# Six chunks instead of four for the prompt alone in the first gated MLP, and a wider pace for the sample stream

## The chip, the cores and the metric

The kernel runs on one core of one Trainium2 chip. Its engines work side by side, each in the order in which its own instructions stand: PE (TensorE, matrix products), DVE (VectorE), ACT (ScalarE), POOL (GpSimd) and SP (SyncE, which issues most of the transfers). Transfers run on 16 DMA engines that all queues share. The metric is the device time of one execution in microseconds (us); less is better.

## The reference

A two-layer decoder trunk is run over a prompt of 512 tokens and over 8 sample sequences of 8 new tokens each (64 rows), with the same weights. Layer 0 has stick-breaking attention, in which the samples also attend to 2048 cached positions in pages of 128; layer 1 has a diagonal complex state-space layer (S5). Both end in a gated MLP with a causal convolution of width 3.

```python
def trunk(x, past_kv, ssm_prev, conv_prev, p):
    ...
        h = rms_norm(x, p["norm_mix"][i])
        if i % 2 == 0:
            y, k, v = attn_mixer(h, ..., past_k, past_v)      # samples: 16 pages of 128 keys each
        else:
            y, fr, fi = s5_mixer(h, ...)
        x = x + y
        h = rms_norm(x, p["norm_ffn"][i])
        y, cs = conv_ffn(h, w_up, conv_w, conv_b, w_down, prev)
        x = x + y

def conv_ffn(h, w_up, conv_w, conv_b, w_down, prev):
    a, b = jnp.split(h @ w_up, 2, axis=-1)                    # (rows, 2816) each
    padded = jnp.concatenate([prev, a], axis=1)
    c = conv_b + conv_w[0] * padded[:, 0:s] + ...             # width 3
    return (silu(c) * b) @ w_down, padded[:, s:]
```

D_MODEL is 1024 and D_FF 2816, so an MLP has 22 chunks of 128 hidden features.

## The kernel before, in words

**Precision.** A product in float32 is made of three float32r products: weights (`whi`, `wlo`) and activations (`hT`, `g`, `o_hi` and `o_lo`) are split into a high and a low part. A weight unit of 128x1024 is loaded by SP into one of three `raw` buffers (`load_unit`, L150); ACT copies it to `whi` (L139) and DVE subtracts to get `wlo` (L140). Four pairs of them form a ring.

**The stream.** `sample_cache` (L396) walks over the cached pages of the samples, two sequences at a time, in 64 steps. A step loads two pages of keys (`kp`, SP's queue, two buffers) and of values (`vp`, POOL's queue, two buffers), turns the keys on DVE (`kt`, L427), makes the scores on PE (`z`, L448), turns the weights (`z<-ident,sg`, L473) and multiplies with the values (`po`, L483). Each step is four pieces. `accompany(stream, WEAVE)` puts one piece behind every 2400 cycles of products; `tick`, which every product loop calls, counts them. This sets the place of a piece in the program. The program is then ordered by a list scheduler: each engine takes what the scheduler holds ready, earlier program text first, so pieces can move ahead of their place where an engine would be idle, and fall back to their place where it is full.

**The stages.** Queries are projected for all heads; then eight pairs of heads are projected, normed and attended (`project_pair`, `norm_pair`, `prompt_pair`); then the attention output is multiplied with `w_o` for the prompt (`psg<-w,o`, 192 products of 512 columns); then comes the first MLP, `ffn(0, ...)`. The stream runs beside all of them.

**The first MLP.** `PLAN0` lists its groups as (both, first chunk, number of chunks). A group multiplies its chunks up (`up`, products of L880 to L882 into `up` or, for the first parts of chunks 0 and 1, into `dn`), and then down (`gemm`, L267 to L269, into `dn`, four prompt tiles of 128 rows times two halves of the output). Where `both` is false the group holds the 512 prompt columns alone, because the samples' rows are not there yet. During its down products `sample_joins` is run: the stream is finished, the new tokens are attended (`sample_new`: `psc`, `zn`, `pwn`, `pon`, `pot`), their attention output `soT` is multiplied with `w_o` (`pso`, 32 products), added and normed, and turned into `hT` and `sT` (`up<-ident,h` with 64 rows). Chunks of later groups hold 576 columns, prompt and samples. The samples' part of the first chunks is made up later by `sample_group`, with the samples as the stationary operand and the weights, loaded a second time, as the moving one; its pieces are taken one behind each chunk from chunk `SSTART` on. Beside the later chunks runs the preparation of the S5 layer (`s5_prepare`, "aside"), mostly DVE and POOL work in steps, `ASTEPS` (44) of them spread by `beside` over the chunks up to `AEND` (20).

Lines to know: L139 and L140 splits; L880 to L882 up products; L267 to L269 down products; L264 and L265 products with the samples as stationary operand; L1031 the samples' up products of `sample_group`; L219 transposes into `hT`.

Of the kernel before, what the change touches and what calls it, by code (L numbers as in the profile page):

```python
# [9 lines left out]
F32 = mybir.dt.float32  # L10
F32R = mybir.dt.float32r
# [3 lines left out]
ALU = mybir.AluOpType  # L15
AX = mybir.AxisListType

P = 128
# [3 lines left out]
NT = SEQ // P  # L22
DB = 8
# [20 lines left out]
GUNITS = 0, 2, 4, 6  # L44
WEAVE, NPERIOD, IPERIOD = 2400, 6000, 1200
BIG = 4
ASTEPS, AEND = 44, 20
SSTART = 14
GROUPS = [[4], [0, 1], [2, 3]]
# [14 lines left out]
AHEAD = 2  # L64
PLAN0 = [(False, 0, 4), (True, 4, 6), (True, 10, 4), (True, 14, 4), (True, 18, 4)]
PLAN1 = [(True, 0, 6), (True, 6, 6), (True, 12, 6), (True, 18, 4)]
# [25 lines left out]
def hybrid_kernel(  # L92
# [179 lines left out]
    def sample_rows(pool, ps, out, tag, bufs):  # L272

        lo = pool.tile([P, 512], F32, name="slo", tag=tag, bufs=bufs)
        S.copy(lo[:NS], ps[NS:2 * NS])
        V.tensor_tensor(out, ps[:NS], lo[:NS], ALU.add)

# [632 lines left out]
    def ffn(l, start, plan, then=None, between=None, aside=None):  # L910
# [3 lines left out]
        with ExitStack() as fctx:  # L914
            pool = fctx.enter_context(pool_(name=f"ffn{l}", bufs=2))
            ups = fctx.enter_context(pool_(name=f"ffn{l}_u", bufs=2, space=PSUM))
            dps = fctx.enter_context(pool_(name=f"ffn{l}_d", bufs=3, space=PSUM))
            extra = {}

            def bank():  # L920
# [35 lines left out]
            def beside(ins, c):  # L956

                with tc.issue_after(ins.ins), tc.issue_after(last_mm["PE"].ins):
                    while steps["n"] * (AEND - plan[1][1]) < ASTEPS * (c - plan[1][1]):
                        next(steps["of"], None)  # L960
                        steps["n"] += 1
# [56 lines left out]

            def sample_group(sx, sT, c0):

                cs = slice(c0, c0 + 4)
                out = []
                for part in range(2):
                    f0 = part * FF + c0 * P
                    ps = down_bank(3)
# [9 lines left out]
                    sample_rows(pool, ps, t[:NS], "cv", 2)  # L1035
                    ps = down_bank(3)
                    for c in range(4):
                        T.transpose(ps[:, c * NS:(c + 1) * NS], t[:NS, c * P:(c + 1) * P], ident[:NS, :NS])
                    src = ps[:, :4 * NS].rearrange("p (c b s) -> p c b s", c=4, s=DS)
                    if part == 0:  # L1040
                        ap = pool.tile([P, 4, DB, 2 + DS], F32, name="sap", tag="apad")
                        for c in range(4):
                            G.tensor_copy(ap[:, c, :, 0:2], hist[:, :, c0 + c].rearrange("p (b j) -> p b j", j=2))
                        S.copy(ap[:, :, :, 2:], src)
                        for c in range(4):
                            G.tensor_copy(cst[:, 2:, c0 + c].rearrange("p (b j) -> p b j", j=2), ap[:, c, :, DS:])
                        cv = sx.tile([P, 4, DB, DS], F32, name="scv", tag="scv")
                        t = pool.tile([P, 4, DB, DS], F32, name="sct", tag="cv")

                        def per(w):  # L1050
                            return cw[:, w, cs, None, None].to_broadcast([P, 4, DB, DS])

# [7 lines left out]
                V.tensor_tensor(cv, src, cv, ALU.mult)  # L1060
                g = sx.tile([P, 4, P], F32R, name="sg", tag="sg2")
# [40 lines left out]
            def sample_joins():  # L1102
# [15 lines left out]
                aside_ps = fctx.enter_context(pool_(name="aside_ps", bufs=1, space=PSUM, side="right"))  # L1118
                yield (chain(*(sample_group(sx, sT, c) for both, c, _ in plan if not both)),
                        aside(fctx.enter_context(pool_(name="aside", bufs=2, side="right")),  # L1120
                              lambda: aside_ps.tile([P, 512], F32, name="as", tag="as")))

            for both, c0, ncg in plan:
# [15 lines left out]
                if not both:  # L1139
                    joining = sample_joins()  # L1140
                    x = next(joining)
                    for n in range(2):
                        units = down_units(c0, ncg, n)
                        for i in range(NT):
                            if (n, i) in JOINAT:
                                x = next(joining)
                            ps = down_bank(0)
                            gemm([(i, ps)], lhs, units, 2, ncg)
                            add(i, ps, halves[n], False)
                    early, steps["of"] = x  # L1150
                elif last:
# [612 lines left out]
```

## Time and profile before

| what | value |
|---|---|
| time of the runs, median of 3 | 1870.84 us (1863.1 to 1871.09) |
| time of the profiled execution | 1861.24 us |
| its span from first to last instruction | 1859.6 us, so 1.6 us lie around it |
| PE busy, share of the span | 1696.9 us, 91% |
| DVE busy | 1157.4 us, 62% |
| ACT busy | 740.9 us, 40% |
| POOL busy | 279.4 us, 15% |
| moved by DMA | 297.30 MB, 160 GB/s in the mean |

Busy PE is not PE at its peak: the records of matmuls overlap, and the clock that the chip grants PE changes (PEclk, in shares of 2.4 GHz). So shares over the whole span say little here; the stages differ, and the rows below are read stage by stage.

### The profile page before, as it was taken

The page shows a single profiled execution, that of the slowest core. Times are in us where ns is not written, and L with a number is a line of the kernel's source. Part 1 is how long each engine was busy: PE and PEld are TensorE (multiplying, and loading weights), DVE is VectorE, ACT ScalarE, POOL GpSimd, SP SyncE. Part 2 cuts the span into 40 slices and gives each one's busy share as a digit, 9 for nine tenths or more (in the row PEclk, how much of TensorE's full clock was granted, in tenths as well). Part 3 has the DMA queues.
Part 4 walks back from the last instruction along what each step waited for, and adds up shares of the span by engine and source line. Part 5 has one row for each costly group of instructions (what it writes and reads, how often), then busy time and mean ns, then how long its engine had stood idle before and what let it go on. Part 6 is the DMA issues. An engine that isn't in the chain of part 4 may idle for free. (4 is left out here: it accounts for less than half of the span.)

```text
span 1859.6 us, 34131 instructions
## 1 busy us (share of the span) xinstructions
PE 1696.9 (91%) x12765; PEld 1425.3 (77%) x12765; DVE 1157.4 (62%) x2132; ACT 740.9 (40%) x1526; POOL 279.4 (15%) x455
## 2 busy tenths in 40 slices
PE   5979878898788879997999899899999999999999
PEld 4867655566445668796888889789888989989897
DVE  7356755676775567799577887665446544444443
ACT  4324443454453336433244534454433423323231
POOL 3011000111111100066032332011010100000000
PEclk8989988898788989999999999999999999999999
DMA  8399989999999973623375736455322222232221
GB/s 250 97 251 267 252 213 252 257 254 264 275 257 257 255 191 95 181 69 117 113 146 150 199 108 172 120 161 169 118 82 73 91 81 80 81 91 80 82 80 64
DMA packets 278713, 297.30 MB, mean 160 GB/s; under 512 B 54424, under 2 KB 197745, under 8 KB 278548
## 3 DMA queue, kind: packets, MB, share of 16 engines
q1 hardware_dynamic: 258642, 226.66, 45.7%
q0 software_dynamic: 18752, 67.41, 12.9%
q8 instruction: 101, 1.65, 0.4%
q10 hardware_dynamic: 1154, 1.05, 0.2%
q14 instruction: 64, 0.52, 0.1%
HBM read 268.93 MB, written 26.13 MB: 159 GB/s over the span
## 5 line engine op out<-in xcount | busy, mean ns | idle before, releaser
L880 PE MATMUL up<-hT,whi 128*128 128x256 f32 (+2 forms) x1344 | 406.7, 303 | 14.1 <-DVE gf L1000 5.4
L140 DVE TENSOR_TENSOR wlo<-raw,whi 128x1024 fp32r<-128x1024 f32 x203 | 255.2, 1260 | 254.8 <-ACT whi L139 239.4
L881 PE MATMUL up<-hT,whi 128*128 128x256 f32 (+2 forms) x1344 | 402.9, 300 | 0.0
L882 PE MATMUL up<-hT,wlo 128*128 128x256 f32 (+2 forms) x1344 | 402.8, 300 | 0.0
L139 ACT CAST whi<-raw 128x1024 fp32r<-128x1024 f32 x206 | 215.5, 1049 | 335.5 <-PE up L881 152.3
L880 PEld LDWEIGHTS up<-hT,whi 128*128 128x128 f32 x1344 | 256.3, 191 | 22.4 <-DVE gf L1000 7.1
L881 PEld LDWEIGHTS up<-hT,whi 128*128 128x128 f32 x1344 | 256.5, 191 | 3.6 <-issue 0.8
L882 PEld LDWEIGHTS up<-hT,wlo 128*128 128x128 f32 x1344 | 256.2, 191 | 1.6 <-issue 0.2
L427 DVE STREAM_TRANSPOSE kt<-kp 128x1024 f32<-128x1024 f32 x128 | 152.2, 1224 | 156.0 <-DMA kp<-in_cache_k_dram 131.9
L422 POOL DMA_DIRECT2D vp<-in_cache_v_dram x128 | 67.8, 530 | 572.1 <-PE po L483 447.7
L267 PE MATMUL dn<-whi,g 128*128 128x512 f32 x352 | 137.3, 401 | 9.3 <-DVE xres L1077 5.3
L268 PE MATMUL dn<-wlo,g 128*128 128x512 f32 x352 | 140.6, 400 | 0.0
L269 PE MATMUL dn<-whi,g 128*128 128x512 f32 x352 | 139.0, 398 | 0.0
L448 PE MATMUL z<-kt,Qall 128*32 128x128 f32 x2048 | 89.0, 305 | 52.2 <-DVE kt L427 46.6
L448 PEld LDWEIGHTS z<-kt,Qall 128*32 128x32 f32 x2048 | 61.2, 121 | 77.7 <-issue 38.0
L986 POOL COPY cst<-apad 128x2 f32<-128x2 f32 x44 | 39.3, 894 | 510.3 <-ACT apad L974 510.3
L267 PE MATMUL psg<-whi,hT 128*128 128x256 f32 (+1 forms) x320 | 103.2, 325 | 0.0
L268 PE MATMUL psg<-wlo,hT 128*128 128x256 f32 (+1 forms) x320 | 101.9, 319 | 0.0
L269 PE MATMUL psg<-whi,hT 128*128 128x256 f32 (+1 forms) x320 | 100.7, 318 | 0.0
L457 ACT ACTIVATE left<-z,nbias_r 128x128 f32<-128x128 f32 x128 | 40.1, 364 | 146.8 <-PE z L448 128.8
L483 PE MATMUL po<-vp,wT 128*32 128x256 f32 x1024 | 79.8, 432 | 16.5 <-DMA vp<-in_cache_v_dram 11.9
L267 PEld LDWEIGHTS dn<-whi,g 128*128 128x128 f32 x352 | 66.2, 189 | 27.0 <-DVE xres L1077 6.2
(484 smaller groups left out, 3329.9 us busy)
## 6 DMA issues: line engine op xcount, KB each, us to landing
kp<-in_cache_k_dram SPq DMA_DIRECT2D x256, 256.0 KB, 9.1
vp<-in_cache_v_dram POOLq DMA_DIRECT2D x128, 512.0 KB, 9.2
raw<-in_ffn_w_up_dram SPq DMA_DIRECT2D x96, 512.0 KB, 4.4
raw<-in_ffn_w_down_dram SPq DMA_DIRECT2D x48, 512.0 KB, 3.3
raw<-in_attn_w_qkv_dram SPq DMA_DIRECT2D x64, 128.0 KB, 3.6
raw<-in_attn_w_o_dram SPq DMA_DIRECT2D x16, 512.0 KB, 5.4
raw<-in_ssm_w_glu_dram SPq DMA_DIRECT2D x32, 256.0 KB, 3.3
f_scr<-ca SPq DMA_DIRECT2D x8, 512.0 KB
```

Source lines behind the costliest of these rows:

```text
L139: S.copy(hi, src)
L140: eng.tensor_tensor(lo, src, hi.bitcast(F32), ALU.subtract)
L267: T.matmul(ps, x[0], whi, start=st, stop=False)
L268: T.matmul(ps, x[0], wlo, start=False, stop=False)
L269: T.matmul(ps, x[1], whi, start=False, stop=sp_)
L422: last_dma[G] = G.dma_start(vps[i][:, s], cache_v[0, bass.ds(r, 1)].rearrange("o k h d -> (o k) (h d)"))
L427: V.transpose(kts[i, a].rearrange("p b c k -> p b (c k)"), kps[i][:, :, a * 256:(a + 1) * 256])
L448: T.matmul(z[32 * h:32 * h + 32, a * P:(a + 1) * P].rearrange("p (k b) -> p b k", b=4), Qall[:, b, 8 * a + 2 * h + half, :], kt[:, :, 2 * ...
L483: T.matmul(po[32 * h:32 * h + 32, a].rearrange("p (s j d) -> p s j d", s=2, j=2), wT[:, a, 32 * h:32 * h + 32], v[:, a, h], start=m0 == NP ...
L880: T.matmul(ps[:, :t1 - t0], w[0][:, k, :], hi, start=k == 0, stop=False)
L881: T.matmul(ps[:, :t1 - t0], w[0][:, k, :], lo, start=False, stop=False)
L882: last_mm["PE"] = T.matmul(ps[:, :t1 - t0], w[1][:, k, :], hi, start=False, stop=k == KC - 1)
```

## The change

`PLAN0` gets a second group for the prompt alone, chunks 4 and 5; the first group for both starts at chunk 6 and has four chunks. The samples join in the last group for the prompt alone (`joins`). `sample_group` takes the number of its chunks as an argument, so that a group of two is made up as well, with weight units of half the size. A piece of the stream is put behind every 2900 cycles of products instead of 2400. The pieces of `sample_group` are taken from chunk 9 on instead of 14. The 44 steps beside the chunks are counted from chunk 6 instead of 4, and so stand beside 14 chunks instead of 16.

```diff
-WEAVE, NPERIOD, IPERIOD = 2400, 6000, 1200
+WEAVE, NPERIOD, IPERIOD = 2900, 6000, 1200
-SSTART = 14
+SSTART = 9
-PLAN0 = [(False, 0, 4), (True, 4, 6), (True, 10, 4), (True, 14, 4), (True, 18, 4)]
+PLAN0 = [(False, 0, 4), (False, 4, 2), (True, 6, 4), (True, 10, 4), (True, 14, 4), (True, 18, 4)]
...
+            first_both = min(c for both, c, _ in plan if both)
...
-                    while steps["n"] * (AEND - plan[1][1]) < ASTEPS * (c - plan[1][1]):
+                    while steps["n"] * (AEND - first_both) < ASTEPS * (c - first_both):
...
-            def sample_group(sx, sT, c0):
+            def sample_group(sx, sT, c0, m4):
...
-                        w = rows_unit(ffn_w_up[l], u * 256, 2, f0, 512)
+                        w = rows_unit(ffn_w_up[l], u * 256, 2, f0, m4 * P)
...
-                    gemm([(NT, ps)], lambda k, i: g[:, k], down_units(c0, 4, n), 2, 4)
+                    gemm([(NT, ps)], lambda k, i: g[:, k], down_units(c0, m4, n), 2, m4)
...
                 if not both:
-                    joining = sample_joins()
-                    x = next(joining)
+
+                    joins = c0 == max(c for b, c, _ in plan if not b)
+                    if joins:
+                        joining = sample_joins()
+                        x = next(joining)
                     for n in range(2):
                         units = down_units(c0, ncg, n)
                         for i in range(NT):
-                            if (n, i) in JOINAT:
+                            if joins and (n, i) in JOINAT:
                                 x = next(joining)
                             ps = down_bank(0)
                             gemm([(i, ps)], lhs, units, 2, ncg)
                             add(i, ps, halves[n], False)
-                    early, steps["of"] = x
+                    if joins:
+                        early, steps["of"] = x
```

**What it moves.** The lines of the changed kernel are one higher from L275 on, and more further down (z is L449 there, po L484). On every engine the order is the same as before until about the 34th step of the stream, in the middle of the pairs. The first place is PE in the middle of the products with `w_o`. Before, a step of the stream stood between any two dozen of them:

```order
L269 MATMUL psg<-whi,o_lo 128x512
L267 MATMUL psg<-whi,o_hi 128x512
L483 MATMUL po<-vp,wT 32x256 x8
L448 MATMUL z<-kt,Qall 32x4x32 x16
L473 MATMUL z<-ident,sg 128x128 x2
L268 MATMUL psg<-wlo,o_hi 128x512
L269 MATMUL psg<-whi,o_lo 128x512
```

Now all 192 of them follow each other but for a few rows at their beginning and their end; these are the end:

```order
L269 MATMUL psg<-whi,o_lo 128x512
L484 MATMUL po<-vp,wT 32x256 x3
L449 MATMUL z<-kt,Qall 32x4x32 x16
L474 MATMUL z<-ident,sg 128x128 x2
L484 MATMUL po<-vp,wT 32x256 x8
L908 MATMUL up<-ident,nat 128x88
L881 MATMUL dn<-hT,whi 128x256
```

Counted over PE's whole order, 53 of the 64 `po` steps stood ahead of the products with `w_o` before, nine more ahead of the first MLP's first product (seven of them among the products with `w_o`), and the last two beside chunk 0. Now 52 stand ahead of `w_o`, one is cut in two among its products (five rows of eight, and the three that are seen above), one comes behind them, and ten follow the first MLP's first product, spread over the up products of chunks 0 to 3 and the down products of the first group. The last of them comes just ahead of chunk 4.

DVE shows the same place by the adds of the products with `w_o` into the residual rows (`xres`). Before, the stream's key turns and scans stood between them:

```order
L140 TENSOR_TENSOR wlo<-raw,whi 128x1024
L818 TENSOR_TENSOR xres_91<-psg,xres_91 128x512
L427 STREAM_TRANSPOSE kt<-kp 128x1024 x2
L463 SCALAR_TENSOR_TENSOR left<-left 128x129 x2
L818 TENSOR_TENSOR xres_92<-psg,xres_92 128x512
```

Now there are none:

```order
L140 TENSOR_TENSOR wlo<-raw,whi 128x1024 x2
L819 TENSOR_TENSOR xres_91<-psg,xres_91 128x512
L819 TENSOR_TENSOR xres_92<-psg,xres_92 128x512
L819 TENSOR_TENSOR xres_93<-psg,xres_93 128x512
L819 TENSOR_TENSOR xres_94<-psg,xres_94 128x512
```

The second place is PE where the samples join: `pot` turns their attention output, `pso` multiplies it with `w_o`, `dn` are down products of the group in which they join. Before, 18 down products stood between the last `pot` and the first `pso`, and the `pso` came by fours among the down products:

```order
L269 MATMUL dn<-whi,g 128x512
L264 MATMUL pso<-whi,soT 128x512
L265 MATMUL pso<-wlo,soT 128x512
L264 MATMUL pso<-whi,soT 128x512
L265 MATMUL pso<-wlo,soT 128x512
L267 MATMUL dn<-whi,g 128x512
```

Now the group has half as many down products; the last `pot` is followed at once by all 32 `pso`, and 24 down products are left behind them, before the samples' rows are turned:

```order
L268 MATMUL dn<-wlo,g 128x512
L269 MATMUL dn<-whi,g 128x512
L570 MATMUL pot<-ident,osum 128x128 x4
L264 MATMUL pso<-whi,soT 128x512
L265 MATMUL pso<-wlo,soT 128x512
L264 MATMUL pso<-whi,soT 128x512
```

## Rows read from the trace of the kernel before

**Rows 1.** Stretches: from:to, length, busy (count) PE, PEld, DVE, ACT, POOL, clock, DMA, GB/s
```profile
466.00:584.00 118.00, 92.57 (x929) 51.44 (x929) 79.46 (x139) 51.06 (x135) 14.26 (x27) 0.79 1.00 266
...
593.70:625.90 32.20, 32.20 (x301) 24.55 (x300) 20.67 (x32) 11.92 (x32) 4.23 (x8) 1.00 1.08 259
...
668.00:685.00 17.00, 16.64 (x151) 14.31 (x151) 6.81 (x29) 2.55 (x8) 0.89 (x4) 0.83 0.47 135
...
783.80:796.80 13.00, 13.00 (x99) 12.94 (x98) 11.62 (x53) 4.91 (x11) 2.11 (x6) 1.00 0.28 83
...
795.00:890.00 95.00, 81.85 (x502) 74.12 (x501) 89.75 (x198) 29.71 (x45) 58.65 (x73) 0.95 0.32 103
890.00:1190.00 300.00, 284.80 (x1862) 255.90 (x1860) 220.26 (x340) 129.72 (x236) 78.04 (x87) 0.99 0.55 141
```

**Rows 2.** PE in order of time, the stream's value products at the end of the pairs
```profile
566.12 1.07 PE L483 MATMUL po<-vp,wT 128*32 128x256 f32 x16 [2.25 <-DMA vp<-in_cache_v_dram]
...
575.12 1.94 PE L483 MATMUL po<-vp,wT 128*32 128x256 f32 x16
```

**Rows 3.** PE in order of time, steps of the stream around products with w_o
```profile
584.01 0.78 PE L267 MATMUL psg<-whi,o_hi 128*128 128x512 f32 x1
...
601.83 1.07 PE L483 MATMUL po<-vp,wT 128*32 128x256 f32 x16
602.72 1.06 PE L448 MATMUL z<-kt,Qall 128*32 128x128 f32 x32
603.70 0.44 PE L473 MATMUL z<-ident,sg 128*128 128x128 f32 x2
...
604.45 0.39 PE L269 MATMUL psg<-whi,o_lo 128*128 128x512 f32 x1
...
609.58 0.39 PE L267 MATMUL psg<-whi,o_hi 128*128 128x512 f32 x1
609.90 1.07 PE L483 MATMUL po<-vp,wT 128*32 128x256 f32 x16
...
653.97 1.91 PE L219 MATMUL psg<-ident,h 128*128 128x128 f32 x8
655.53 0.78 PE L267 MATMUL psg<-whi,o_hi 128*128 128x512 f32 x1
...
659.20 1.05 PE L448 MATMUL z<-kt,Qall 128*32 128x128 f32 x32
...
665.37 1.93 PE L483 MATMUL po<-vp,wT 128*32 128x256 f32 x16 [3.82 <-ACT wT L475]
```

**Rows 4.** PE in order of time, landmarks of the first MLP
```profile
668.34 0.56 PE L880 MATMUL dn<-hT,whi 128*128 128x256 f32 x1
...
756.91 0.40 PE L265 MATMUL pso<-wlo,soT 128*128 128x512 f32 x1
...
768.70 0.71 PE L219 MATMUL up<-ident,h 64*128 64x64 f32 x8 [0.38 <-DVE h L210]
...
1190.79 0.42 PE L880 MATMUL vy<-hT,whi 128*128 128x320 f32 x1 [1.40 <-DVE hT L140]
```

**Rows 5.** PE in order of time, first and last of 24 up products of 256 columns
```profile
845.42 0.28 PE L880 MATMUL up<-hT,whi 128*128 128x256 f32 x1
...
848.18 0.28 PE L882 MATMUL up<-hT,wlo 128*128 128x256 f32 x1
```

**Rows 6.** Groups by form, 684.5:769 us: busy us, mean ns | idle before, releaser
```profile
L140 DVE TENSOR_TENSOR wlo<-raw,whi 128x1024 fp32r<-128x1024 f32 x19 | 23.1, 1221 | 8.9 <-ACT whi L139 8.9
```

**Rows 7.** The same by form, DVE alone, 795:890 us
```profile
L140 DVE TENSOR_TENSOR wlo<-raw,whi 128x1024 fp32r<-128x1024 f32 x12 | 18.1, 1511 | 2.0 <-ACT whi L139 2.0
```

**Rows 8.** The page, transfers: count, KB each, median us from issue to landing
```profile
kp<-in_cache_k_dram SPq DMA_DIRECT2D x256, 256.0 KB, 9.1
vp<-in_cache_v_dram POOLq DMA_DIRECT2D x128, 512.0 KB, 9.2
raw<-in_ffn_w_up_dram SPq DMA_DIRECT2D x96, 512.0 KB, 4.4
```

More of the change, by code (lines that the diff above doesn't have):

```diff
@@ L272, in sample_rows @@
     def sample_rows(pool, ps, out, tag, bufs):
+        n = ps.shape[-1]
         lo = pool.tile([P, 512], F32, name="slo", tag=tag, bufs=bufs)
-        S.copy(lo[:NS], ps[NS:2 * NS])
-        V.tensor_tensor(out, ps[:NS], lo[:NS], ALU.add)
+        S.copy(lo[:NS, :n], ps[NS:2 * NS])
+        V.tensor_tensor(out, ps[:NS], lo[:NS, :n], ALU.add)
     def tiles_of(xT):
@@ L1017, in up @@
                 yield g
-            def sample_group(sx, sT, c0):
-                cs = slice(c0, c0 + 4)
+            def sample_group(sx, sT, c0, m4):
+                cs = slice(c0, c0 + m4)
                 out = []
@@ L1024, in sample_group @@
                     f0 = part * FF + c0 * P
-                    ps = down_bank(3)
+                    ps = down_bank(3)[:, :m4 * P]
                     for u in range(4):
-                        w = rows_unit(ffn_w_up[l], u * 256, 2, f0, 512)
+                        w = rows_unit(ffn_w_up[l], u * 256, 2, f0, m4 * P)
                         for a in range(2):
@@ L1034, in sample_group @@
                     t = pool.tile([P, 512], F32, name="srow", tag="cv")
-                    sample_rows(pool, ps, t[:NS], "cv", 2)
+                    sample_rows(pool, ps, t[:NS, :m4 * P], "cv", 2)
                     ps = down_bank(3)
-                    for c in range(4):
+                    for c in range(m4):
                         T.transpose(ps[:, c * NS:(c + 1) * NS], t[:NS, c * P:(c + 1) * P], ident[:NS, :NS])
-                    src = ps[:, :4 * NS].rearrange("p (c b s) -> p c b s", c=4, s=DS)
+                    src = ps[:, :m4 * NS].rearrange("p (c b s) -> p c b s", c=m4, s=DS)
                     if part == 0:
-                        ap = pool.tile([P, 4, DB, 2 + DS], F32, name="sap", tag="apad")
-                        for c in range(4):
+                        ap = pool.tile([P, m4, DB, 2 + DS], F32, name="sap", tag="apad")
+                        for c in range(m4):
                             G.tensor_copy(ap[:, c, :, 0:2], hist[:, :, c0 + c].rearrange("p (b j) -> p b j", j=2))
                         S.copy(ap[:, :, :, 2:], src)
-                        for c in range(4):
+                        for c in range(m4):
                             G.tensor_copy(cst[:, 2:, c0 + c].rearrange("p (b j) -> p b j", j=2), ap[:, c, :, DS:])
-                        cv = sx.tile([P, 4, DB, DS], F32, name="scv", tag="scv")
-                        t = pool.tile([P, 4, DB, DS], F32, name="sct", tag="cv")
+                        cv = sx.tile([P, m4, DB, DS], F32, name="scv", tag="scv")
+                        t = pool.tile([P, m4, DB, DS], F32, name="sct", tag="cv")
                         def per(w):
-                            return cw[:, w, cs, None, None].to_broadcast([P, 4, DB, DS])
+                            return cw[:, w, cs, None, None].to_broadcast([P, m4, DB, DS])
                         V.tensor_tensor(cv, ap[:, :, :, 0:DS], per(0), ALU.mult)
@@ L1060, in sample_group @@
                 V.tensor_tensor(cv, src, cv, ALU.mult)
-                g = sx.tile([P, 4, P], F32R, name="sg", tag="sg2")
+                g = sx.tile([P, m4, P], F32R, name="sg", tag="sg2")
                 split(g[:, :, :NS], g[:, :, NS:], cv.rearrange("p c b s -> p c (b s)"))
@@ L1118, in sample_joins @@
                 aside_ps = fctx.enter_context(pool_(name="aside_ps", bufs=1, space=PSUM, side="right"))
-                yield (chain(*(sample_group(sx, sT, c) for both, c, _ in plan if not both)),
+                yield (chain(*(sample_group(sx, sT, c, n) for both, c, n in plan if not both)),
                         aside(fctx.enter_context(pool_(name="aside", bufs=2, side="right")),
```

## The prediction

> **What bounds the kernel now.** I read the busy time, the clock and the DMA share stretch by stretch, then PE in order of time at the places where a stage begins or ends, then DVE by groups where PE waits for it, and last the table of transfers.
>
> In the last part of the pairs PE is busy for 92.57 of 118 us at a clock of 0.79, while the DMA share is 1.00 at 266 GB/s [rows 1]. A value product waits there for its page [rows 2]. So pages set the pace. The same holds beside the products with `w_o`: DMA share 1.08 at 259 GB/s [rows 1], and a step of the stream comes each 609.90 - 601.83 = 8.07 us [rows 3]. A step needs four transfers of 256 KB and two of 512 KB [rows 8], 2.1 MB, and 2.1 MB in 8.07 us are 260 GB/s. But here PE is full as well (32.20 of 32.20 us, clock 1.00), so the stream costs PE only its own work: 1.07 + 1.06 + 0.44 = 2.57 us a step [rows 3].
>
> Behind the stream PE is the bound (13.00 of 13.00 us in one chunk for both, [rows 1]) but for one stretch: from 795 to 890 DVE is busy for 89.75 of 95 us and PE for 81.85. That is where the S5 preparation runs beside the chunks.
>
> **The change, part by part.** Prices of products: of 512 columns 0.233 us (604.45 to 609.58 are 22 intervals, [rows 3]), of 256 columns 0.12 us (845.42 to 848.18, 23 intervals, [rows 5]). I follow four places on PE.
>
> *A, where the pairs end.* On all engines the order is the same as before up to about step 34, so nothing moves there. Then the wider pace puts one step fewer ahead of `w_o`. In the pairs a step costs what its pages cost, 575.12 - 566.12 = 9.0 us [rows 2], not its 2.57 us of PE work. `w_o` began at 584.0 [rows 3]; now 575.0. Bounds: 2.57 us, if the prompt's own chain is what ends the pairs, and 13.5 us, since one and a half key steps are gone. I take 9, as the row shows PE waiting for that page.
>
> *B, the products with `w_o`.* They lose the stream: 192 x 0.233 = 44.7 us, one value product 1.1, and 16 transposes. Eight of these took 655.53 - 653.97 = 1.56 us, so 3.1. The end stays as it was: `z`, its weights turned, and a value product that waited 3.82 us for ACT, with nothing on PE to fill it. From that `z` at 659.20 [rows 3] to the first MLP product at 668.34 [rows 4] are 9.1 us. Together 58.0 us, so the first MLP begins at 633.0 instead of 668.3. What ends here is also a stretch in which the DMA engines were full: the two key buffers and two value buffers fill and then wait for 45 us.
>
> *C, from the first MLP's start to the samples' transposes.* Before: 768.70 - 668.34 = 100.4 us [rows 4]. Added are 96 up products of chunks 4 and 5 (22.4 us), 48 more down products (11.2 us), and eight more steps of the stream, ten instead of two (8 x 2.57 = 20.6 us). That gives 154.6 us if nothing waits that didn't wait before. Four new waits come on top:
> - The last `pot` is followed at once by the first `pso`. The 18 down products that stood between are gone, 18 x 0.233 = 4.2 us, and `pso` needs `soT` copied by ACT and split by DVE. I take 4.2; below, 0.
> - 32 `pso` in a row use eight weight units. Four pairs can be ready; each further one costs DVE 1.22 us [rows 6] against 4 x 0.233 = 0.93 us on PE. I take 1; bounds 0 and 8 x 0.29 = 2.3.
> - From the end of the last `pso` (756.91 + 0.40) to the transposes at 768.70 passed 11.4 us, the samples' adds and norm, and PE waited only 0.38 of it [rows 4], since down products filled the rest. Now 24 stand there, 5.6 us. So 5.8 us are uncovered. Queued behind the waiting transposes are all up products of chunk 6, which hold the samples' columns; nothing can go ahead.
> - The stream needs pages again. The first steps in chunks 0 and 1 follow each other after 24 products of 256 columns, 2.9 + 2.57 us and some transposes, say 6.3 us, where pages allow one in 8.07. Three such steps lack 5.3 us; later steps have 25 products of 512 columns between them, 5.8 + 2.57 = 8.4 us, but MLP weights want the same DMA engines. Over the whole: about 16 MB of pages not yet in buffers and 6 MB of weights in 96 us (46 of chunks 0 to 3, 22 down, 26 stream, 2 transposes) are 230 GB/s, under the 259 seen. I take 6; bounds 0 and 20 (rival 2).
>
> C is 154.6 + 4.2 + 1 + 5.8 + 6 = 171.6 us, and the transposes come at 633.0 + 171.6 = 804.6 instead of 768.7.
>
> The Trainium skill (DMA: Bandwidth & Descriptors, Bandwidth) gives about 358 GB/s as the limit from memory to one core; by it the 22 MB would take an estimated 61 us, and the term of 6 us would be 0. The trace disagrees: share 1.00 at 266 GB/s [rows 1].
>
> *D, the chunks for both.* Before they took 1190.79 - 768.70 = 422.1 us [rows 4]. Two of 18 leave: an up part of 13.1 us (96 products of the 99 in the 13.00 us of [rows 1], with their starts) and 28 down products, 6.5 us; twice 19.6 is 39.3 us. The samples' part of chunks 4 and 5 is added: 32 products of 256 columns, 8 of 512, and turns, 3.8 + 1.9 + 0.7 = 6.4 us. The 44 steps of the S5 preparation stand beside 14 chunks instead of 16. Where DVE is the bound, from 795 to 890, the work that leaves PE gives nothing back: at most 95 x (1 - 14/16) = 11.9 us. At least 0, since from 890 on DVE has room (220.26 of 300 us, [rows 1]). I take 3, near the low end, because the spread is over all chunks and the tight stretch holds four of them. D is 422.1 - 39.3 + 6.4 + 3 = 392.2 us.
>
> One cost in this stretch has a rule beside it. A split into `wlo` took 1.22 us [rows 6] and 1.51 us among POOL's work [rows 7]; the samples' extra units now begin at chunk 9, so more of them may be split beside POOL, at 0.29 us each for some 18 units: 5 us of DVE, inside the bound above. The Trainium skill (SBUF — State Buffer, SBUF: two separate sides) says that the port pair that DVE and GpSimd share is an exclusive lock. By it a blocked split would wait out the whole POOL instruction; the rows agree in direction, with 24% in the mean.
>
> *Sum.* The layer behind the first MLP begins at 804.6 + 392.2 = 1196.8 instead of 1190.8: +6.0 us. From there on the order is the same. The profiled execution took 1861.2 (span 1859.6 and 1.6 around it), so 1867.2. The median of the runs is 1870.8, 9.6 us above it, and one of the three runs lies at 1863.1; by the median it would be 1876.8. I take the middle of the two, 1872.
>
> Seen from the other side: PE's own work hardly changes (6.4 us more for the samples, 2 x 2.8 us less in the two chunks). The change trades waits: 6 us of pages in the pairs and about as much beside `w_o` go, 17 us in the first MLP and 3 in D come.
>
> **Rivals.** A measurement of this kernel can tell about 0.5%, 9.3 us, from no change.
>
> 1. *Faster: the empty DMA stretch pays.* During `w_o` buffers fill, so the ten steps find their pages and wait for nothing (-6); PE comes out of `w_o` without the idle end (0.85 and 3.82 us go, -4.7) and so without the clock of 0.83 that it had for 17 us after it [rows 1] (-2.9); `soT` and the weights come early (-5.2); the preparation costs nothing (-3). From +6.0 that is -15.8, and with the upper bound of A -20. For it: 230 is below 259 GB/s. Against it: only two steps' pages fit the buffers. Time 1846. It decides when at least 15.3 of these 26 us are saved.
> 2. *Slower: the first MLP waits for pages, and the clock falls with it.* Steps and weights together want more than 260 GB/s in parts of chunks 0 to 3; PE stands in order behind `z` and `po`, as in the pairs, and its clock goes to what such a stretch shows, 0.83 [rows 1]: 96/0.83 = 116, so 20 us instead of 6. That is +20, time 1886. It decides as soon as the stream's waits pass 9.3 us, 1 us a step.
> 3. *Slower: DVE sets the pace in D.* The 3 us become 12, and the samples' splits wait beside POOL: +15, time 1881. For it: DVE at 89.75 of 95 us. Against it: nothing of this holds from 890 on.
> 4. *Nothing in sum.* `pot` and `pso` have other work ahead of them by the time their operands are late (-5.2) and the stream waits 2 us instead of 6: -3, time 1863.
>
> **How the numbers follow.** The sum as it stands 0.42 (its own range, from the small bounds, -6 to +18: no measurable change 0.26, slower 0.15, faster 0.01); rival 1 0.22 (faster 0.21, same 0.01); rival 2 0.15 (slower 0.14, same 0.01); rival 3 0.08 (slower 0.07, same 0.01); rival 4 0.13 (same 0.11, faster 0.02). That makes faster 0.24, same 0.40, slower 0.36. The range leaves out the better half of rival 1 and the worse third of rival 2: 1850 to 1892.
>
> **What would show it.** In the profile after: `w_o` begins near 575 (A); the first `dn<-hT` near 633 (B), with a wait for `wT` just ahead of it, and DMA shares far below 1 in the 45 us before; the last `po` near 735, with waits for `kt` or `vp` of together 6 us; a first `pso` some 4 us after the last `pot`; turns of the samples' rows near 805 that wait 5 to 6 us for `h`; the next layer's first product near 1197. Wrong it would be if the pairs end two steps sooner or not at all, if the granted clock between 633 and 735 falls under 0.9 (rival 2) or stays at 1.00 without waits (rival 1), if PE's idle time in D grows by more than 10 us (rival 3), or if a stage behind 1200, which I hold to be unchanged, moves by more than 5 us.

## The result and the profile after

The changed kernel took 1889.76 us (median of 4 runs, 1883.03 to 1896.38), the kernel before 1870.71 us in the same session; the ratio is 1.0111 (95% interval 1.0067 to 1.0156). It is slower by about 1.1%. The profiled execution's span is 1881.4 us instead of 1859.6. The median lies near the upper end of the range on record, 18 us above the predicted 1872.

The stretches of the changed kernel, cut at the four places of the prediction (columns as in [rows 1]); 997.5 is where chunk 14 begins:

```profile
466.00:571.50 105.50, 75.70 (x806) 43.22 (x806) 70.07 (x126) 46.08 (x124) 12.73 (x24) 0.85 0.98 244
571.50:626.00 54.50, 52.46 (x295) 40.30 (x292) 35.56 (x73) 21.07 (x44) 1.06 (x2) 0.98 0.63 163
626.00:668.00 42.00, 35.25 (x372) 29.77 (x372) 26.15 (x56) 14.60 (x34) 5.53 (x12) 0.94 1.04 253
668.00:727.00 59.00, 58.98 (x488) 44.37 (x489) 38.40 (x58) 30.21 (x53) 7.60 (x16) 1.00 0.85 236
727.00:796.00 69.00, 56.07 (x410) 42.46 (x408) 52.34 (x117) 35.17 (x62) 2.15 (x6) 0.89 0.48 142
796.00:997.50 201.50, 167.84 (x1030) 153.70 (x1031) 158.94 (x336) 70.75 (x114) 82.91 (x105) 0.91 0.48 127
997.50:1211.70 214.20, 199.43 (x1319) 178.77 (x1318) 164.09 (x267) 94.73 (x183) 59.30 (x59) 0.98 0.52 137
```

Beside the products with `w_o` (the second row) the DMA share fell to 0.63, since the stream is gone from there. In the next 42 us it is 1.04, and PE is idle for 6.75 us; 2.9 us of these are waits of `z` for turned keys, and DVE itself had waited for their pages (6.05 and 5.57 us, at 643 and 653 us). In the two rows of the chunks for both PE is busy for 367.3 of 415.7 us.

The landmarks of the changed kernel on PE, in order of time, which answer to [rows 3, 4]:

```profile
571.49 0.50 PE L267 MATMUL psg<-whi,o_hi 128*128 128x512 f32 x1
...
624.07 1.88 PE L484 MATMUL po<-vp,wT 128*32 128x256 f32 x16 [2.04 <-ACT wT L476]
...
626.00 0.56 PE L881 MATMUL dn<-hT,whi 128*128 128x256 f32 x1
...
725.55 1.07 PE L484 MATMUL po<-vp,wT 128*32 128x256 f32 x16
...
767.24 0.56 PE L264 MATMUL pso<-whi,soT 128*128 128x512 f32 x1 [2.44 <-DVE soT L140]
...
771.94 0.80 PE L264 MATMUL pso<-whi,soT 128*128 128x512 f32 x1 [2.86 <-DVE soT L140]
...
796.22 1.11 PE L219 MATMUL up<-ident,h 64*128 64x64 f32 x8 [4.92 <-DVE h L210]
...
1211.70 0.64 PE L881 MATMUL vy<-hT,whi 128*128 128x320 f32 x1 [1.40 <-DVE hT L140]
```

Set against the prediction's places, in us of one profile each:

| place | before | predicted | after |
|---|---|---|---|
| A, `w_o` begins | 584.0 | 575.0 | 571.5 |
| B, from there to the first MLP | 84.3 | 58.0 | 54.5 |
| C, to the samples' transposes | 100.4 | 171.6 | 170.2 |
| D, the chunks for both | 422.1 | 392.2 | 415.5 |
| from the next layer's first product to PE's last | 665.0 | 665.0 | 666.0 |

A, B and C came out within 3.5 us each. D was to give back 29.9 us and gave 6.6. The whole of D, first in the kernel before, then in the changed one:

```profile
768.70:1190.79 422.09, 392.43 (x2552) 354.97 (x2552) 329.52 (x600) 169.55 (x299) 139.35 (x167) 0.98 0.50 132
796.22:1211.70 415.48, 367.27 (x2348) 332.47 (x2348) 322.88 (x601) 165.49 (x297) 142.21 (x163) 0.94 0.50 132
```

PE's idle time in it grew from 29.7 to 48.2 us, and the granted clock over it was 0.94 instead of 0.98.

What PE waited for most between 796 and 1212, longest waits of the changed kernel (line, releaser, us in total, times, longest):

```profile
PE up L881 <- DVE gf L1002: 9.7, 3, 6.6
PE dn L267 <- DVE xres L1079: 8.8, 1, 8.8
PE as L1422 <- ACT es L1461: 7.8, 1, 7.8
PE dn L1033 <- DVE wlo L140: 7.3, 1, 7.3
```

The longest waits end at 873, 911, 937 and 989 us, while chunks 9 to 13 are worked on. The first three end with DVE's work, the last, a product of the S5 preparation, with ACT's. `L1033` is a samples' up product that waits for its weights to be split. In the kernel before the largest single wait of this stage was 5.1 us.

### The profile page after: what moved, and what is told of

The parts are those of the page before. It is cut to its first block, busy times and chain, and to the rows that moved or that the text cites. A ratio compares the mean times of both kernels' runs of the same rounds, so it can differ in the third digit from the quotient of the medians.

```text
span 1881.4 us, 34079 instructions
## 1 busy us (share of the span) xinstructions
PE 1696.4 (90%) x12705; PEld 1423.2 (76%) x12705; DVE 1172.8 (62%) x2158; ACT 756.4 (40%) x1545; POOL 284.6 (15%) x455
## 5 line engine op out<-in xcount | busy, mean ns | idle before, releaser
L140 DVE TENSOR_TENSOR wlo<-raw,whi 128x1024 fp32r<-128x1024 f32 x213 | 261.8, 1232 | 256.2 <-ACT whi L139 243.3
L881 PE MATMUL up<-hT,whi 128*128 128x256 f32 (+2 forms) x1312 | 403.2, 307 | 13.1 <-DVE gf L1002 9.7
L883 PE MATMUL up<-hT,wlo 128*128 128x256 f32 (+2 forms) x1312 | 398.6, 304 | 0.0
L139 ACT CAST whi<-raw 128x1024 fp32r<-128x1024 f32 (+1 forms) x216 | 222.3, 1033 | 352.2 <-PE up L882 172.9
L881 PEld LDWEIGHTS up<-hT,whi 128*128 128x128 f32 x1312 | 253.7, 193 | 22.0 <-DVE gf L1002 10.7
L882 PEld LDWEIGHTS up<-hT,whi 128*128 128x128 f32 x1312 | 253.5, 193 | 4.0 <-issue 0.4
L423 POOL DMA_DIRECT2D vp<-in_cache_v_dram x128 | 68.1, 532 | 585.3 <-PE po L484 466.7
L267 PE MATMUL dn<-whi,g 128*128 128x512 f32 x352 | 139.5, 401 | 10.2 <-DVE xres L1079 8.8
L449 PE MATMUL z<-kt,Qall 128*32 128x128 f32 x2048 | 89.3, 299 | 48.3 <-DVE kt L428 45.3
L988 POOL COPY cst<-apad 128x2 f32<-128x2 f32 x44 | 45.3, 1029 | 524.0 <-ACT apad L976 524.0
L449 PEld LDWEIGHTS z<-kt,Qall 128*32 128x32 f32 x2048 | 60.4, 118 | 73.6 <-issue 39.5
L267 PE MATMUL psg<-whi,hT 128*128 128x256 f32 (+1 forms) x320 | 103.5, 326 | 0.0
L484 PE MATMUL po<-vp,wT 128*32 128x256 f32 x1024 | 78.0, 420 | 15.1 <-DMA vp<-in_cache_v_dram 10.3
```

The costliest lines, as they stand in the source:

```text
L139: S.copy(hi, src)
L140: eng.tensor_tensor(lo, src, hi.bitcast(F32), ALU.subtract)
L267: T.matmul(ps, x[0], whi, start=st, stop=False)
L423: last_dma[G] = G.dma_start(vps[i][:, s], cache_v[0, bass.ds(r, 1)].rearrange("o k h d -> (o k) (h d)"))
L449: T.matmul(z[32 * h:32 * h + 32, a * P:(a + 1) * P].rearrange("p (k b) -> p b k", b=4), Qall[:, b, 8 * a + 2 * h + half, :], kt[:, :, 2 * ...
L484: T.matmul(po[32 * h:32 * h + 32, a].rearrange("p (s j d) -> p s j d", s=2, j=2), wT[:, a, 32 * h:32 * h + 32], v[:, a, h], start=m0 == NP ...
```

## The experiments

All ratios are to the kernel before, measured in the same session on the same chip. Two theories are about D. S: the samples' pieces, taken from chunk 9 on, meet the S5 preparation on DVE. D: the preparation itself is denser beside 14 chunks. (The first experiment has a third, also called J there: the clock alone.) Two are about the pace. P: a stream step taken out of the pairs saves its pages and costs PE's 2.57 us elsewhere. N or J: it is waited for elsewhere, or the stream's end holds up the samples.

**The samples' pieces from chunk 14 on.** The changed kernel with

```diff
-SSTART = 9
+SSTART = 14
```

> The changed kernel with the samples' groups taken from chunk 14 on, as before the change, instead of 9; four of their twelve pieces are then left for the end of the MLP. Between the samples' transposes (796.2 us in the changed kernel) and the next layer's first product (1211.7) lie 415.5 us, where 392 were forecast. Theory S (the samples' units, begun at chunk 9, meet the dense part of the S5 preparation on DVE, and PE waits for weight pairs and adds): this stretch falls by 12 to 20 us, to about 400, and PE's waits between 900 and 980 go; the time falls by as much less some 4 us for the four pieces at the end. Theory D (44 steps of the preparation beside 14 chunks instead of 16 are what DVE cannot do in time): it stays above 408. Theory J (the chunks for both lose nothing, the clock does): stays at 415.

1879.01 us, ratio 1.0075 (1.0034 to 1.0116). D is 407.8 us. Up to chunk 14 it took 171.8 us where the changed kernel took 201.3; behind it 236.0 instead of 214.2, with four pieces drained one behind the other at the end. So 29.5 us went and 21.8 came back. S gave 12 to 20 us for the whole stretch; it fell by 7.7, to just under the 408 from which on D would have held, and did not stay at 415 as by the clock alone. Not decided between S and D.

**Two pieces behind each chunk from 14 on.** As above, and

```diff
                     if both and c >= SSTART:
                         next(early, None)
+                        next(early, None)
```

> The changed kernel with the samples' pieces taken two behind each chunk from chunk 14 on, instead of one from chunk 9 on; none is left for the end. Without the groups the stretch of the chunks for both took 384.3 us in the new plan; the pieces of chunks 9 to 13 made 29 us of it in the changed kernel (16.7 us of products), those from chunk 14 on only 2.2 (9.8 us of products). Theory S (pieces are cheap once the dense part of the S5 preparation is over): the stretch is 392 to 402 us, and the time 13 to 23 us below that of the changed kernel, about 0.1 to 0.4% above before. Rival (pieces cost their products, and more where two stand together): 408 to 416, the time of the changed kernel or that with one piece from chunk 14 on.

1872.74 us, ratio 1.0045 (1.0021 to 1.0070). D is 400.3 us, inside what S gave (392 to 402) and clear of the rival's 408 to 416. Its two halves, cut at chunk 14 (972 us):

```profile
801.30:972.00 170.70, 155.41 (x983) 144.14 (x983) 136.82 (x310) 57.46 (x98) 77.00 (x91) 0.94 0.41 104
972.00:1201.60 229.60, 212.35 (x1367) 188.73 (x1367) 184.71 (x290) 108.46 (x200) 74.72 (x73) 0.96 0.60 162
```

Set beside the two last rows of the stretches above: the same chunks 6 to 13 take 170.7 us instead of 201.5, DVE has 136.8 us to do instead of 158.9, and POOL 77.0 instead of 82.9. All twelve pieces lie in the second half, which grew by 15.4 us. The whole of D in this version:

```profile
801.28:1201.56 400.28, 367.74 (x2348) 332.85 (x2348) 321.49 (x599) 165.92 (x297) 151.72 (x163) 0.95 0.52 137
```

PE has the same 2348 products as in the changed kernel and is busy for the same time, 367.7 and 367.3 us. So the 15.2 us by which D fell are PE's idle time, 32.5 us instead of 48.2: what the early place of the pieces costs is waits.

**Without the samples' groups, new plan and old.** Both kernels leave out the samples' part of the chunks that run for the prompt alone (0 to 5 in the new plan, 0 to 3 in the old). The new plan:

```diff
-                yield (chain(*(sample_group(sx, sT, c, n) for both, c, n in plan if not both)),
+                yield (iter(()),
...
             cst = pool.tile([P, NCV, NFC], F32, name="cst", bufs=1)
+            G.memset(cst, 0.0)
```

> The changed kernel without the samples' groups: the samples' part of chunks 0 to 5 is left out. It is to be read beside the next kernel, the one before without its group (chunks 0 to 3). From the samples' transposes to the next layer the changed kernel took 415.5 us and the one before 422.1, where 29 us less were forecast. Theory S (the samples' pieces taken from chunk 9 on cost more than their products, since they compete with the S5 preparation for DVE): without them the stretch is 415.5 - 26 (products of both groups) - 15 to 25 of waits, 365 to 375. Theory D (the preparation, denser beside 14 chunks, is what is missing): it falls by the products alone, to 385 to 392.

The old plan, with the same edits:

> The kernel before without its samples' group: the samples' part of chunks 0 to 3 is left out. Products of that group are 20 us, and one piece a chunk from chunk 14 on lies where DVE has room. Theory S: the stretch from the samples' transposes to the next layer falls from 422.1 by 20 to 24 us, to 398 to 402, that is 28 to 36 us above the changed kernel without groups (two chunks less are 39.3). Theory D: the same 398 to 402 here, but only 8 to 16 above the changed kernel without groups.

1854.8 us, ratio 0.9966 (0.9922 to 1.0009), and 1855.66 us, ratio 0.9961 (0.9923 to 0.9999). D is 384.3 us in the new plan and 412.3 in the old. The halves of the new plan's, cut at chunk 14:

```profile
800.00:972.00 172.00, 156.08 (x982) 144.79 (x982) 136.74 (x309) 57.13 (x97) 76.72 (x91) 0.94 0.41 103
972.00:1184.00 212.00, 194.14 (x1266) 173.78 (x1266) 147.61 (x240) 83.78 (x165) 59.22 (x61) 0.95 0.50 131
```

and those of the old one's:

```profile
763.40:975.30 211.90, 195.53 (x1256) 179.63 (x1257) 163.84 (x347) 73.01 (x125) 82.57 (x108) 0.96 0.46 116
975.30:1175.70 200.40, 188.52 (x1241) 170.36 (x1239) 140.47 (x228) 80.52 (x156) 53.53 (x51) 0.97 0.46 123
```

Two things follow. Two chunks less are worth 412.3 - 384.3 = 28.0 us, not 39.3: the other 11.3 are lost without any group. They are not lost in the tight stretch alone: the first half has 274 products fewer and is 39.9 us shorter, the second has 25 more and is 11.6 us longer; with the 25 products at 0.233 us taken off, about half of the loss lies behind chunk 14. And the groups cost 422.1 - 412.3 = 9.8 us in the old plan, but 415.5 - 384.3 = 31.2 us in the new. Of these, 201.3 - 172.3 = 29.0 us lie ahead of chunk 14, for five pieces, and 2.2 behind it, for seven. With two pieces behind each chunk from 14 on the groups cost 400.3 - 384.3 = 16.0 us.

The expectations price the groups' products too high, at 20 us for the group of four and 26 or 26.5 for both. Counted in the traces, the group of four is 48 products of 512 columns and 8 turns, 48 x 0.233 + 0.8 = 12.0 us; with the 6.4 us of the group of two both are 18.4, of which 40 products and 8 turns, 10.1 us, lie ahead of chunk 14. So in the new plan the groups cost 12.8 us more than their products, and in the old 2.2 less. By the ranges as written the new plan's 384.3 lies beside D's (385 to 392) and not in S's (365 to 375); with the right price of the products S would have been 372 to 382 and D 397, and 384.3 lies nearer to S. The old plan's 412.3 is in no range, and the difference of 28.0 stands at the end of S's. So both theories hold a part.

**Denser steps in the old plan.** The kernel before with

```diff
-ASTEPS, AEND = 44, 20
+ASTEPS, AEND = 44, 18
```

> The kernel before with the 44 steps of the S5 preparation spread up to chunk 18 instead of 20: beside 14 chunks, as in the changed kernel, with nothing else changed. Theory D (density is what the chunks for both pay for): the stretch from the samples' transposes to the next layer grows from 422.1 by 12 to 20 us and the time with it, about +0.8%. Theory S: it grows by less than 5 us.

1874.18 us, ratio 1.0052 (1.0019 to 1.0086). D is 431.4 us, 9.3 more than before, between the two theories:

```profile
777.69:1209.10 431.41, 396.60 (x2553) 358.63 (x2553) 328.47 (x600) 168.47 (x299) 150.38 (x167) 0.97 0.48 129
```

It agrees with the 11.3 us above: the density alone costs 9 to 11 us. PE's idle time grew by 5.1 us; the other 4.2 are the same products taking longer, 396.6 us busy instead of 392.4, at a clock of 0.97 instead of 0.98.

**The steps of the preparation spread over 16 chunks again.** The changed kernel with

```diff
-ASTEPS, AEND = 44, 20
+ASTEPS, AEND = 44, 22
```

> The changed kernel with the 44 steps of the S5 preparation spread up to chunk 22 instead of 20, so that they stand beside 16 chunks again. Theory D (density of the steps): the stretch of the chunks for both falls from 415.5 to about 400 us, and the time by some 15 us. Theory S (the samples' units at chunk 9): it falls by less than 5 us, since both still stand together. Against both, the preparation's end could now come late for the next layer: then the stretch grows by up to 10 us at its end.

1909.32 us, ratio 1.0253 (1.0183 to 1.0323). D is 435.3 us, 20 more than in the changed kernel; the expectation's last case had the direction, but at most 10 us. The largest wait in it stands at the end of the stage, where the next layer's rows are turned (line, releaser, us in total, times, longest):

```profile
PE up L219 <- DVE h L865: 16.5, 2, 16.3
```

So the last steps, moved behind chunk 20, hold up the next layer. The run says nothing for or against density, since the edit moved the preparation's end as well.

**The old pace with the new plan.** The changed kernel with

```diff
-WEAVE, NPERIOD, IPERIOD = 2900, 6000, 1200
+WEAVE, NPERIOD, IPERIOD = 2400, 6000, 1200
```

> The changed kernel with the old pace, a piece of the stream per 2400 cycles. The stream should stand beside the products with w_o again: these begin near 584 and the first MLP near 668 instead of 571.5 and 626. If the wider pace pays (theory P: pages in the pairs cost 9 to 12.5 us a step, and the steps in the first MLP cost only PE's own 2.57 us), the samples' transposes come 10 to 17 us later than the 796.2 of the changed kernel, near 810, and the whole is 10 to 17 us slower than it, near 1900. If the pace is neutral or loses (theory N: what the pairs give is waited for in the first MLP), they come at 790 to 800 and the time is that of the changed kernel or less. The stretch of the chunks for both stays at 415 +- 5 by either.

1899.10 us, ratio 1.0196 (1.0123 to 1.0269). `w_o` began at 588.2, the first MLP at 672.9, the transposes came at 812.3, and D was 415.8 us: what P gave. By the ratios it is 0.85% slower than the changed kernel, some 16 us, but their intervals overlap. All of this is A: from `w_o` to the transposes both kernels took the same, 224.1 and 224.7 us, so what eight steps fewer gave in the first MLP, they cost beside `w_o`. And A scatters, as the section on the prediction shows.

**The new pace with the old plan.** The kernel before with

```diff
-WEAVE, NPERIOD, IPERIOD = 2400, 6000, 1200
+WEAVE, NPERIOD, IPERIOD = 2900, 6000, 1200
```

> The kernel before with the new pace alone (2900), the old plan and the old start of the samples' groups. Theory P: products with w_o near 571.5, first MLP near 626, then 100.4 us as before and eight steps of 2.57 us more, some waits: transposes at 750 to 757 instead of 768.7, the chunks for both 422 as before, so 12 to 18 us faster than before, about 1849 in a profile. Rival (the stream now ends too late for the group in which the samples join, so that the new tokens' attention, with its products by w_o and norm, has too few products beside it): the transposes come at 765 to 775, and the time is that of before within 0.5%.

1874.81 us, ratio 1.0045 (1.0003 to 1.0087). P failed here. The profile is that of the longest of ten executions, 1886.54 us; `w_o` began in it at 585.3, not near 571.5. From `w_o` to the first MLP it took 54.3 us and D 422.9, but C took 151.9 us, where the old C and PE's own work of eight steps make 100.4 + 8 x 2.57 = 121.0. PE's idle time in C is 30.2 us (6.8 before) and its clock 0.85 (0.96). The longest wait in C (same columns):

```profile
PE psc L381 <- ACT perm L372: 10.4, 1, 10.4
```

With the last value product at 733 and the transposes at 791.5, the samples' chain behind the stream lay bare: its first product `psc` waited, and so did those behind it. In the changed kernel two more chunks stand beside this chain.

**The stream taken out of the pairs but kept beside `w_o`.** Three versions of the kernel before set the pace anew where the products with `w_o` begin. With A for the pace in the pairs and B for that from `w_o` on:

```diff
-WEAVE, NPERIOD, IPERIOD = 2400, 6000, 1200
+WEAVE, NPERIOD, IPERIOD = A, 6000, 1200
...
         following = norm_next(norm_ffn[0])
+        streaming[0]["period"] = B
+        streaming[0]["left"] = min(streaming[0]["left"], B)
```

A is 3200 and B is 800 in the first:

> The kernel before with a pace of 3200 in the pairs and of 800 from the products with w_o on. PE's order then has 48 steps of the stream ahead of w_o instead of 53, seven among its products as before, one behind them and eight instead of two in the first MLP. If pages set the pace of the pairs (theory P), five steps fewer bring w_o forward by 40 to 60 us, to 525 to 545 from the start; with a start that late in the first MLP the samples join some 25 to 45 us later against its start, and the whole is 5 to 25 us faster than before. If the prompt's own chain ends the pairs (rival), five steps give their PE work alone, 13 us, w_o begins near 571, and the whole is 10 to 30 us slower.

2900 and 300 in the second:

> The kernel before with a pace of 2900 in the pairs and of 300 from the products with w_o on: 52 steps of the stream ahead of w_o instead of 53, seven among its products as before, two behind them and three in the first MLP, where two were. If a step in the pairs costs its pages, 8 to 9 us, and in the first MLP PE's 2.57 us alone (theory P), w_o begins some 8 us earlier, the samples join 5 to 6 us earlier, and the time is 0.2 to 0.4% below that of before. If the stream's end is what the samples wait for (theory J), they join no earlier and the time is that of before.

3050 and 300 in the third:

> The kernel before with a pace of 3050 in the pairs and of 300 from the products with w_o on: 50 steps ahead of w_o instead of 53, seven among its products, one behind them and six in the first MLP instead of two. With 8.2 us for the first step and 5.4 for each, as the earlier runs give in the mean (53 steps: w_o at 588; 52: 580; 48: 561), w_o begins 16 to 20 us earlier. Theory P: the first MLP's stretch up to the samples' transposes, 100.4 us, grows by four steps of 2.57 us and 3 to 5 us of waits, and the whole is 4 to 8 us faster than before. Theory J: the samples' chain needs 57 us behind the last step in both runs with a late stream, so a last step at 700 or later puts the transposes at 757 or later, and the gain is 0 to 4 us.

| steps ahead of `w_o` / in the first MLP | `w_o` begins | `w_o` to first MLP | C | D | time, ratio to before |
|---|---|---|---|---|---|
| 53 / 2 (before) | 584.0 | 84.3 | 100.4 | 422.1 | 1 |
| 52 / 3 | 561.5 | 90.1 | 103.5 | 421.9 | 1867.53 us, 1.0007 (0.9981 to 1.0034) |
| 50 / 6 | 569.0 | 75.0 | 133.0 | 421.7 | 1877.48 us, 1.0058 (1.0033 to 1.0084) |
| 48 / 8 | 561.2 | 77.0 | 136.7 | 422.5 | 1866.83 us, 1.0016 (0.9988 to 1.0044) |

`w_o` begins earlier in all three, but not in the order of the steps: up to there the version with 52 has the changed kernel's order, and its 561.5 is the lowest of seven such profiles (mean 577.4). With 48 steps it began at 561.2, between what P (525 to 545) and the rival (571) gave. Where six or eight steps follow, C gives the gain back: four steps more cost 32.6 us instead of 10.3, six more 36.3 instead of 15.4. In the kernel with six the longest of PE's single waits in C is for turned keys (same columns):

```profile
PE z L448 <- DVE kt L427: 5.4, 1, 5.4
```

DVE had waited 5.1 us for that page, so a step that no longer waits for its pages in the pairs can wait for them in the first MLP. But this is the smaller part: such waits are 5.4 us with six steps and 3.1 with eight, of the 22 and 21 us that C grew beyond PE's own work. The rest are waits of the samples' chain (`pso` 9.0 and 6.3 us, 1.4 before) and for weights, and a clock of 0.87 and 0.88 instead of 0.96. One step moved made no difference that the runs can tell. P gave a gain for all three, and none came; J gave none for the second and 0 to 4 us for the third, but that one was slower by 0.6%. The first was slower by 0.16%, where its rival gave 10 to 30 us. None of the versions beats the kernel before.

## Why the prediction was right, and where it failed

**What came true.** The forecast was a slower kernel within what can be told, +6 us; it is +19 us by the medians, in the range, on the forecast's side. The chance of 0.36 for slower covers it, the likeliest case doesn't. That it is in the range is in part luck: the sum's own bounds ended at +18, and the range went to 1892 for rival 2, whose clock wasn't seen (0.94 and 1.00 between 626 and 727).

**A** was priced at one step of pages, 9.0 us. Up to `w_o` PE's order is the same in the changed kernel and in six of the versions: those with the pieces late, two pieces, steps to 22 and no groups, the old plan with the new pace, and that with 52 steps and a pace of 300 from `w_o` on. In these seven `w_o` began at 571.5, 587.8, 579.9, 578.0, 577.5, 585.3 and 561.5 us. In the kernel before and three versions with its order it began at 584.0, 588.2, 582.4 and 598.4. The means are 577.4 and 588.2: some 11 us apart, with 26 and 16 us of scatter within. So the mean is near the price, but the runs can't tell 9 us from half or twice of it, and the changed kernel's 571.5 is in part luck.

**B** was 3.5 us too long, half of it because the value product at its end waited 2.04 us for ACT instead of 3.82.

**C** was right in its sum, and its four waits together nearly so, 17.2 us for 17.0. `pso` waited 2.44 + 2.86 us for `soT` and 2.73 for `srow` (4.2 forecast), the transposes 4.92 us for `h` (5.8), the stream 2.9 us for keys and 1.4 for `wT` (6). The weight units' 1 us didn't show. With the old pace C took 139.4 us, so eight more steps cost 170.2 - 139.4 = 30.8 us, 20.6 of them PE's own work; ahead of the first MLP, beside `w_o`, the same edit gave 84.7 - 54.5 = 30.2. With the new pace in the old plan C took 151.9, so two more chunks, 33.6 us of products, cost 18.3: the other 15 stand in time in which PE waited there or ran at the lower clock. By the limit of about 358 GB/s that the Trainium skill gives (DMA: Bandwidth & Descriptors, Bandwidth) the stream's term would have been 0; the keys' waits are there, at a share of 1.04 and 253 GB/s.

**D is the step that failed**, in two of its terms. "32 products of 256 columns, 8 of 512, and turns" were to be all that the samples' part adds, 6.4 us; it added 31.2 - 9.8 = 21.4 us. I had priced the second group's products and taken the first group's place for nothing, though its start moved from chunk 14 to 9, into the stretch that I had named as DVE's. That it is the place, the version with two pieces from chunk 14 on shows: the same products, 15.2 us less, all of it PE's idle time. "I take 3" for the density was 9.3 (in the old plan) to 11.3 us (without groups), near the upper bound of 11.9; the reason given for the low end, that the tight stretch holds only four chunks, was wrong, since half of the loss lay behind chunk 14. 15.0 and 8.3 us too little make the 23.3 us by which D missed. (The 13.1 us of an up part are a little high: 96 of the 99 products in 13.00 us are 12.6. With that the density cost 10.2 us without groups, nearer to the other figure.)

The prediction's own sign of rival 3 (DVE sets the pace in D, +15 us) came true: PE's idle time in D grew by 18.6 us, and over 10 was named as a sign of being wrong. Its price fell short: it had D 9 us above the sum, and D came 23.3 above. Its first half, the density, is borne out. Its second, splits that wait beside POOL, is small: 17 splits of 1.36 us instead of 1.28 in the rows below are 1.4 us. And "nothing of this holds from 890 on" was wrong, with waits that end at 911, 937 and 989 us. The same stretch of 104 us, first in the changed kernel, then without groups:

```profile
848.00:952.00 104.00, 81.07 (x454) 72.70 (x454) 88.73 (x133) 34.94 (x50) 51.26 (x56) 0.89 0.40 124
```

```profile
852.00:956.00 104.00, 89.40 (x536) 81.62 (x535) 89.44 (x136) 33.02 (x54) 56.75 (x48) 0.92 0.40 108
```

DVE is as busy in both, 85 and 86% of the time, so not full in the mean; with the samples' pieces among its work PE is busy for 8.3 us less. DVE by groups with their forms, in the same stretch of the changed kernel and at its place in the version with two pieces from chunk 14 on (busy us, mean ns | idle before, releaser):

```profile
L140 DVE TENSOR_TENSOR wlo<-raw,whi 128x1024 fp32r<-128x1024 f32 x17 | 22.9, 1363 | 5.5 <-ACT whi L139 5.5
```

```profile
L140 DVE TENSOR_TENSOR wlo<-raw,whi 128x1024 fp32r<-128x1024 f32 x12 | 15.4, 1283 | 9.0 <-ACT whi L139 8.9
```

Five more splits, 7.5 us of DVE, are the samples' units. That the pieces cost more where they stand early is shown by the runs that move them; that it is by these splits, rather than by the places that the scheduler then gives to everything else, is argued from these rows alone and stays open. A split takes 1.28 to 1.36 us here, between the 1.22 of [rows 6] and the 1.51 of [rows 7]; this agrees in direction only with the exclusive lock that the Trainium skill describes (SBUF — State Buffer, SBUF: two separate sides).

**In sum:** one profile gives A -12.5, B -29.8, C +69.8, D -6.6 and +1.0 behind it, +21.9. Had D come out as forecast, it would have been 1.4 us below the kernel before.

## What to carry to other kernels

Work that is moved has to be priced on every engine at the place where it lands: here the samples' group of four cost 9.8 us for 12.0 us of products where its pieces began at chunk 14, and the pieces that ran from chunk 9 on, among DVE's preparation of the next layer, cost 29.0 us for 10.1 us of products. Before a spread is made denser, or a start earlier, list each engine's busy time in the stretch that receives it. Waits also have a second price: behind them the same products took longer at the lower clock. And steps that a transfer paces are not made cheap by moving them: eight steps cost 30.8 us in the first MLP, 20.6 of them PE's own work, and gave as much ahead of it.

## What the runs showed of the hardware

PE's granted clock was 1.00 from 760 to 766 us. Then PE waited 2.44 us for the first `pso`, and already the products behind this wait came every 0.43 us instead of 0.233; a second wait of 2.86 us followed. The stretch around them in the changed kernel, five microseconds of it behind the second wait, and two of its products:

```profile
766.00:786.00 20.00, 13.17 (x35) 9.43 (x35) 12.37 (x24) 10.45 (x21) 0.00 (x0) 0.66 0.49 148
772.00:777.00 5.00, 5.00 (x12) 3.74 (x12) 2.22 (x4) 2.43 (x4) 0.00 (x0) 0.50 0.36 107
```

```profile
772.54 0.63 PE L265 MATMUL pso<-wlo,soT 128*128 128x512 f32 x1
772.96 0.63 PE L264 MATMUL pso<-whi,soT 128*128 128x512 f32 x1
```

0.50 is the lower of the two levels, 1.2 GHz, in a stretch in which PE was busy throughout; the 0.66 mixes both. Ten products between 772.5 and 776.8 us cost about 2 us more than at the full clock, and eight more from 781.2 us on, behind the wait of 2.73 us, another 1.5. The sum had no term for it; that C came out right nonetheless, since waits that had stood in C before were gone, is luck.

The other thing is the scatter of a stretch in which the DMA engines are full: with the same order on PE, the products with `w_o` began between 561.5 and 587.8 us in seven profiles, at a DMA share of 0.98 to 1.00 and 246 to 259 GB/s between 116 us and there. A change of one step there can't be told in one profile, while D repeated to about 1 us (415.5 and 415.8; 421.7 to 422.9 in five).
